# Second mixer: high parts of most weights written by rounding transfers, and the turns of a tile's last head moved into the projection ahead of it

## The chip, the cores and the metric

The kernel runs on one core of one Trainium2 chip. The metric is the time of one execution on the device, in microseconds; of several runs the median counts. The engines of a core are named as in its profile: PE is TensorE's matmul and PEld its loading of weights (PE's stationary operand), DVE is VectorE, ACT is ScalarE, POOL is GpSimd, and SP is SyncE, which here only issues transfers. Every engine works through its own queue of instructions; semaphores tie the queues together.

## The reference

Two groups of requests, 256 and 512 rows of width 1024, go through the same two layers. Layer 0 mixes the tokens by windowed attention, layer 1 by differential attention, and each mixer is followed by a SwiGLU part. Norms stand before and behind every part. Cut to what matters here, the second mixer is:

```python
def diff_attention(h, w_in, w_o, ..., subln_g, lambda_init):
    qkv = h @ w_in                                  # 1024 x 3072
    q, k, v = split(qkv)                            # 8 heads: two q and k of 64 each, one v of 128
    q, k = apply_rope(q) * HEAD_DIM ** -0.5, apply_rope(k)
    p = softmax(q @ k.T)                            # for both halves of a head
    a = p[:, :, 0] - lam * p[:, :, 1]
    o = rms_norm(a @ v, subln_g) * (1.0 - lambda_init)
    return o @ w_o                                  # 1024 x 1024

x = x + rms_norm(diff_attention(rms_norm(x, g_pre), ...), g_post)
x = x + rms_norm(swiglu(rms_norm(x, ...), ...), ...)
```

Everything is in float32, and all of the keys of a group are seen by each of its queries.

## The kernel before

**Products in two parts.** A float32 product is made of three products in the rounded format fp32r. Each operand is kept as a high part (the value rounded) and a low part (the value less its high part); `product_steps` (L367 on) issues hi x hi, hi x lo and lo x hi into one bank, lines L376 to L378. One step is three matmuls.

**Weights.** A list of units, `units`, names every block of weights in the order of its use, a block being 128 x 1024 in most cases. `plain` (L185) puts a block in the list. `fetch` loads its raw copy (SP, two buffers `wraw`), and `prepare` makes the two parts, `whi` and `wlo`, in rings of five buffers each (`RING`). A high part can come in two ways. Most are made by `two_parts` (L272): ACT casts the raw copy (L273) and DVE subtracts (L274). Units 4 to 13, nine of the first mixer's `waf` and its first block of `wo`, are written by a transfer that POOL issues from the tensor in HBM straight into `whi` (L321); it rounds on the way, and DVE then subtracts as before (L322), from the raw copy that is still loaded. `take` hands out prepared units in order, and `free(n_live)` prepares as many more as the ring holds, each as soon as the last matmul that read its buffer is done. A unit is therefore prepared while four others lie ready or are in use.

**The second mixer**, `mixer_b`. The rows are cut into six tiles of 128, tiles 0 and 1 of the first group and 2 to 5 of the second. `b_fill` lists the products in their order: q and k of a head (two halves of 384 columns each, 24 matmuls a half), and the values in three groups of heads (six tiles each). In the list of units the first q, k and value group come first, then q and k of heads 1 and 2, value group 1 (four units of 128 x 768), q and k of heads 3 to 5, value group 2 (four such units), q and k of heads 6 and 7, then eight units of `wo`, four for each half of its columns. Behind the last use of a unit stands a `drop`, which frees it and prepares another. `rotate` (L653 on) turns the result of a product by rotary positions: ACT copies it out of its bank (L657), POOL swaps neighbouring rows by two transfers (L659), DVE multiplies and adds (L661, L664, L665), and ACT and DVE place the two parts (q: L672, L674; k: L679, L681, and a transfer by POOL at L682). This rest of the work is issued at the end of the next product.

The attention of a head and a tile is three events, set between the steps of the products at places written out by hand: `score` (PE L1017, maxima on DVE L1021, exponentials on ACT L1023, the combination of both softmaxes on DVE L1026 to L1031), two events later `turn_e` (four or two transposes `tpa` on PE L1059, copied by ACT L1061), and one more event later `values` (PE L1072; ACT L1076 scales, L1078 squares). With the last of heads 3, 6 and 7 of a tile the outputs are scaled by their norm on POOL (L421, L1085). `turn_heads` then transposes finished heads for the projection (PE L1043, tile `tp_o`) and splits them in two parts (ACT L1046, DVE L1047); a tile has three such turns, for heads 0 to 3, 4 to 6 and 7.

**The projection.** `out_unit` makes the eight steps of a tile by one half of `wo` and an `end`, which sums squares and applies the gain. In `mixer_b` the last nine scores are interleaved by hand with the steps of tiles 0 to 2 (`run`). Its last entry is the turn of head 7 of tile 3. `project` then does tiles 3 to 5 of the first half, with `turn_o(t + 1)`, the turn of head 7 of the next tile, issued ahead of tile t, and after that all six tiles of the second half, each followed by its norm.

## Time and profile before

| | us |
|---|---|
| three runs | 1639.44, 1642.69, 1642.81 |
| median | 1642.69 |
| the profiled execution | 1643.67 |
| its span, first to last instruction | 1641.9 |
| granted clock of TensorE, mean | 0.998 |

| stage (from the start of the span) | us |
|---|---|
| products of the second mixer, first `pqb` to last `pkb` | 774 to 1050 |
| projection, tiles 0 to 2 with heads 6 and 7 | 1050 to 1093 |
| projection, the rest, and entry of the feed-forward part | 1093 to 1161 |

The page gives busy times by engine over the whole span. A view of stretches gives the same for chosen windows; a view of waits gives, for each engine, which instruction stood idle and what released it; groups put together the instructions of one line and tile; and the timeline gives them one by one: start, length, engine, line, operation, tile written and tiles read, shape, and in brackets the engine's idle time ahead of it with what ended it. A PE row's length holds its passage through the array, so rows overlap; the distance between two starts is what a matmul costs.

### The profile page before, as it was taken

To read this page: it belongs to the slowest core of one execution; us is meant where nothing else is said; L and a number is where in the kernel's file an instruction comes from. 1 tells how busy PE (TensorE), PEld (TensorE's weight loads), DVE (VectorE), ACT (ScalarE), POOL (GpSimd) and SP (SyncE) were. 2 spreads that over 40 slices of the span, in tenths; PEclk is the share of its full clock that TensorE was granted. 3 is DMA by queue.
4 is the path that set the end of the run, shared out by engine and by line. 5 is a ranking of instruction groups with operands and counts; after the bars stand their busy time and mean duration, and the time that the engine had idled before them with its cause. 6 is when DMAs were issued, how large, how long until landed. Compare 5 with 4: busy or idle time off the path is not lost. (4 is left out here: it accounts for less than half of the span.)

```text
span 1641.9 us, 24431 instructions
## 1 busy us (share of the span) xinstructions
PE 1610.2 (98%) x9055; PEld 1491.5 (91%) x9055; DVE 1200.9 (73%) x2076; ACT 941.0 (57%) x1999; POOL 170.9 (10%) x261
## 2 busy tenths in 40 slices
PE   7999999999999999999999999999999999999998
PEld 7888878989999998888999999888999999998887
DVE  6778857886667656988595886847886677656986
ACT  6588976644444444556475666766644444444553
POOL 1121101000000000001220250421000000000000
PEclk9999999999999999999999999999999999999999
DMA  6532204543432347675432332504544332437665
GB/s 213 173 99 68 97 14 170 177 149 133 134 117 97 125 135 251 223 270 179 144 109 73 95 85 79 153 1 164 171 152 141 123 122 96 132 126 255 225 234 175
DMA packets 73383, 233.07 MB, mean 142 GB/s; under 512 B 9072, under 2 KB 17456, under 8 KB 73008
## 3 DMA queue, kind: packets, MB, share of 16 engines
q1 hardware_dynamic: 55008, 178.82, 32.3%
q0 software_dynamic: 18112, 52.44, 10.6%
q8 instruction: 71, 1.16, 0.3%
q14 instruction: 48, 0.39, 0.1%
q10 hardware_dynamic: 144, 0.26, 0.0%
HBM read 171.71 MB, written 42.86 MB: 131 GB/s over the span
## 5 line engine op out<-in xcount | busy, mean ns | idle before, releaser
L274 DVE TENSOR_TENSOR wlo<-wraw,whi 128x1024 fp32r<-128x1024 f32 (+1 forms) x161 | 190.7, 1188 | 188.4 <-ACT whi L273 187.4
L273 ACT CAST whi<-wraw 128x1024 fp32r<-128x1024 f32 (+1 forms) x161 | 164.3, 1024 | 130.7 <-PE py L377 61.5
L376 PE MATMUL py<-hhi,whi 128*128 128x384 f32 x480 | 161.4, 337 | 1.7 <-ACT u L1183 1.2
L378 PE MATMUL py<-hhi,wlo 128*128 128x384 f32 x480 | 160.4, 334 | 0.0
L377 PE MATMUL py<-hlo,whi 128*128 128x384 f32 x480 | 160.4, 334 | 0.0
L364 ACT CAST hhi<-araw 128x768 fp32r<-128x768 f32 (+1 forms) x74 | 57.5, 782 | 94.9 <-DMA araw<-act 94.5
L376 PEld LDWEIGHTS py<-hhi,whi 128*128 128x128 f32 x480 | 90.1, 188 | 4.4 <-ACT u L1183 2.6
L378 PE MATMUL pv<-whi,hlo 128*128 128x512 f32 (+1 forms) x240 | 92.2, 384 | 0.4 <-DVE hlo L365 0.4
L376 PE MATMUL pv<-whi,hhi 128*128 128x512 f32 (+1 forms) x240 | 92.3, 384 | 0.0
L377 PE MATMUL pv<-wlo,hhi 128*128 128x512 f32 (+1 forms) x240 | 92.1, 384 | 0.0
L377 PEld LDWEIGHTS py<-hlo,whi 128*128 128x128 f32 x480 | 90.1, 188 | 0.0
L378 PEld LDWEIGHTS py<-hhi,wlo 128*128 128x128 f32 x480 | 90.1, 188 | 0.0
L365 DVE TENSOR_TENSOR hlo<-araw,hhi 128x768 fp32r<-128x768 f32 (+1 forms) x74 | 65.2, 889 | 34.0 <-ACT hhi L364 33.6
L1226 POOL DMA_DIRECT2D act<-st x22 | 19.3, 879 | 629.4 <-DVE st L1225 599.2
L376 PE MATMUL po<-whi,hhi 128*128 128x512 f32 x192 | 78.5, 409 | 0.0
L1023 ACT ACTIVATE be<-bsc,bmx 128x512 f32<-128x512 f32 (+1 forms) x96 | 58.8, 616 | 29.9 <-DVE bmx L1021 29.5
L377 PE MATMUL px<-hlo,whi 128*128 128x384 f32 x224 | 75.0, 335 | 0.5 <-DVE hlo L365 0.5
L376 PE MATMUL px<-hhi,whi 128*128 128x384 f32 x224 | 75.4, 337 | 0.0
L377 PE MATMUL po<-wlo,hhi 128*128 128x512 f32 x192 | 75.2, 392 | 0.0
L378 PE MATMUL po<-whi,hlo 128*128 128x512 f32 x192 | 75.2, 392 | 0.0
L378 PE MATMUL px<-hhi,wlo 128*128 128x384 f32 x224 | 75.0, 335 | 0.0
L1021 DVE TENSOR_REDUCE bmx<-bsc 128x1 f32<-128x512 f32 (+1 forms) x96 | 55.2, 593 | 11.5 <-PE bsc L1017 11.2
(318 smaller groups left out, 4920.3 us busy)
## 6 DMA issues: line engine op xcount, KB each, us to landing
wraw<-in_wgu SPq DMA_DIRECT2D x60, 512.0 KB, 4.4
act<-st POOLq DMA_DIRECT2D x22, 1344.0 KB, 6.6
araw<-act SPq DMA_DIRECT2D x70, 384.0 KB, 4.0
y_wraw<-in_wgu SPq DMA_DIRECT2D x40, 512.0 KB, 3.6
wraw<-in_wd SPq DMA_DIRECT2D x40, 512.0 KB, 4.0
xd<-x SPq DMA_DIRECT2D x18, 512.0 KB, 2.9
x<-xd SPq DMA_DIRECT2D x18, 512.0 KB, 4.1
wraw<-in_wo SPq DMA_DIRECT2D x16, 512.0 KB, 3.5
```

The source lines that it names most:

```text
L273: state["raw_hi"] = nc.scalar.copy(out=hi, in_=src)
L274: state["raw_lo"] = nc.vector.tensor_tensor(out=lo, in0=src, in1=hi.bitcast(F32), op=ALU.subtract)
L364: state["hi"] = nc.scalar.copy(out=hi, in_=src)
L365: state["lo"] = nc.vector.tensor_tensor(out=lo, in0=src, in1=hi.bitcast(F32), op=ALU.subtract)
L376: nc.tensor.matmul(out, ah, bh, start=start and i == 0, stop=False, skip_group_check=more)
L377: nc.tensor.matmul(out, ah, bl, start=False, stop=False, skip_group_check=more)
L378: state["mm"] = nc.tensor.matmul(out, al, bh, start=False, stop=stop and i == last, skip_group_check=more)
L1021: nc.vector.tensor_reduce(out=mx, in_=s, axis=AX.X, op=ALU.max, negate=True)
L1023: nc.scalar.activation(out=e[:, :n * P], in_=s, func=AF.Exp, bias=mx, accum_out=den[:, c:c + 1])
L1226: nc.gpsimd.dma_start(out=at_hand[c // 4][:, :, c // 2 % 2], in_=out.pop(c // 2))
```

## The change

`plain` takes a flag that puts the unit in a set, `cast`, and `prepare` asks that set instead of the bounds 4 and 14. The flag is set for the first mixer's `waf` and its first `wo` block, as before by the bounds, and now also for `wb` and `wbv` with n > 0 (q and k of heads 1 to 7, value groups 1 and 2) and for the four blocks of the first half of the second mixer's `wo`. In `project` the turn of the next tile's last head is issued behind the first five steps of a tile, not ahead of them; the first mixer passes no such turns.

```diff
-N_PLAIN_A = 14
...
-    def plain(src, n):
+    cast = set()
+
+    def plain(src, n, rounded=False):
+        if rounded:
+            cast.add(len(units))
         units.append(("plain", len(raw_src), n))
         raw_src.append((src, n, "w"))
...
     for f in dict.fromkeys(u for kind, u, _ in a_fill() if kind != "kv"):
-        plain(waf[f], 1024)
+        plain(waf[f], 1024, True)
     for n2 in range(2):
         for i in range(4):
-            plain(wo[0, n2, i], 1024)
+            plain(wo[0, n2, i], 1024, n2 == 0 and i == 0)
...
                 w = 2 * HALF if V_HEADS[n] == 3 else D
-                plain(wbv[n, i, :, :w], w)
+                plain(wbv[n, i, :, :w], w, n > 0)
         else:
-            plain(wb[n, "qk".index(kind)], D)
+            plain(wb[n, "qk".index(kind)], D, n > 0)
     for n2 in range(2):
         for i in range(4):
-            plain(wo[1, n2, i], 1024)
+            plain(wo[1, n2, i], 1024, n2 == 0)
...
-                if 4 <= i < N_PLAIN_A:
+                if i in cast:
                     nc.gpsimd.dma_start(out=hi[:, :n], in_=raw_src[r][0])
...
         for t in range(done, NT):
-            if turn_o is not None and t + 1 < NT:
-                for s in turn_o(t + 1):
-                    s()
-            for s in out_unit(t, wk, o, 0, gp, sq, f"po{layer}_0_{t}"):
+            out = out_unit(t, wk, o, 0, gp, sq, f"po{layer}_0_{t}")
+            for s in out[:5] + (turn_o(t + 1) if turn_o is not None and t + 1 < NT else []) + out[5:]:
                 s()
```

## The prediction

> **What bounds the kernel now.** I read the first part of the page first, then the stretches of time around the second mixer, then who TensorE waited for there.

> ```profile
> span 1641.9 us, 24431 instructions
> PE 1610.2 (98%) x9055; PEld 1491.5 (91%) x9055; DVE 1200.9 (73%) x2076; ACT 941.0 (57%) x1999; POOL 170.9 (10%) x261
> ...
> 774.00:1050.00 276.00, 276.00 (x1759) 269.96 (x1759) 203.73 (x386) 174.98 (x458) 69.27 (x107) 1.00 0.35 102
> 1050.00:1093.00 43.00, 41.53 (x260) 35.31 (x258) 33.85 (x73) 38.21 (x124) 18.40 (x24) 1.00 0.28 82
> ...
> PE tp_h L498 <- DVE y_po L431: 1.4, 1, 1.4
> PE tp_o L1043 <- POOL ob L1085: 1.3, 1, 1.3
> PE tpa L1059 <- ACT be L1023: 0.5, 1, 0.5
> PE tpa L1059 <- ACT aT L1061: 0.5, 1, 0.5
> PE px L377 <- DVE hlo L365: 0.5, 1, 0.5
> PE tpa L1059 <- DVE be L1031: 0.4, 1, 0.4
> ```

> TensorE is busy for 98% of the span, so the end moves only by what TensorE stands idle. The rows of stretches give their length, then the busy time of PE, PEld, DVE, ACT and POOL, the granted clock, and the DMA share. From 774 to 1050 us the second mixer's query, key and value products run with the attention of heads 0 to 5 between them: PE is busy for 276.00 of 276.00 us. From 1050 to 1093 us (heads 6 and 7 among the first three tiles of the output projection; I call it the tail) it idles 1.47 us. The six waits are all that PE had between 770 and 1175 us, in total, times and longest; the second stands behind the tail, in the projection of tiles 3 and 4, the first and the fifth lie behind the projection, at the entry of the feed-forward part. What the change can win is therefore the 1.3 us of `tp_o` and at most the 1.4 us of the three `tpa`.

> **Part one: 26 weights are rounded on the way in.** The new set adds to the second mixer 14 blocks of `wb` (q and k of heads 1 to 7), 8 of `wbv` (groups 1 and 2) and 4 of `wo`. The first mixer keeps its ten: nine `waf` and one `wo`, as with the old bounds 4 to 13. Each of the 26 loses a cast on ACT and gains a transfer issued by POOL; the subtraction on DVE stays (L274 becomes L322).

> ```profile
> L273 ACT CAST whi<-wraw 128x1024 fp32r<-128x1024 f32 x21 | 22.0, 1049 | 12.2 <-PE pvb L378 5.6 <-DMA wraw<-in_wb 2.9 <-PE pqb L377 2.5
> L273 ACT CAST whi<-wraw 128x768 fp32r<-128x768 f32 x8 | 6.7, 832 | 5.3 <-PE pkb L377 4.3 <-PE pqb L377 1.0
> L274 DVE TENSOR_TENSOR wlo<-wraw,whi 128x1024 fp32r<-128x1024 f32 (+1 forms) x29 | 33.1, 1149 | 21.8 <-ACT whi L273 21.6
> ...
> L321 POOL DMA_DIRECT2D whi<-in_waf x9: 530/553/716, 12.6 to 111.6; - x9
>   DVE wlo L322: 5.1, 5
>   PE pqa L376: 0.5, 1
> DMA to landing us min/median/max: 3.8/5.1/5.8
> ```

> The first three rows are groups of 770 to 1060 us (first two) and 770 to 1100 us (third), with count, busy time, mean in ns and idle time before. Of the 29 casts, three stay (two `wbv` of group 0 and the first `wo` of the second half), so ACT loses 18 x 1.049 + 8 x 0.832 = 25.5 us. The value to the end is zero: PE has no idle time in 774 to 1050, where nearly all of these casts lie.

> What part one adds is lateness. The last four rows are the same transfer in the first mixer: 0.553 us to issue, 3.8 to 5.8 us to land, DVE waiting for it or its raw copy 5 times for 5.1 us in all, and PE once for 0.5 us. Before, the wait stood on ACT: 12.2 + 5.3 us of idle time ahead of the casts. Now POOL stands waiting for PE to leave the buffer. Queued behind it there is the rotation's swap of rows of the same product (L659), which waits for that product's end anyway, and then loses only the issue, 0.55 us. Behind the waiting subtraction on DVE stand the maxima (L1021) and combinations (L1031) of the scores, and PE's transposes `tpa` wait for those. How much they can lose:

> ```profile
> 837.32 0.75 DVE L1031 SCALAR_TENSOR_TENSOR be<-be,rho 128x512 f32<-128x512 f32 x1
> 839.17 0.60 PE L1059 MATMUL tpa<-ident,be 128*128 128x128 f32 x4
> ...
> 892.86 0.48 DVE L1031 SCALAR_TENSOR_TENSOR be<-be,rho 128x256 f32<-128x256 f32 x1
> 903.62 0.38 PE L1059 MATMUL tpa<-ident,be 128*128 128x128 f32 x2
> ...
> 1042.48 1.05 ACT L273 CAST whi<-wraw 128x1024 fp32r<-128x1024 f32 x1
> 1051.30 1.03 ACT L273 CAST whi<-wraw 128x1024 fp32r<-128x1024 f32 x1
> 1053.51 0.74 DVE L1031 SCALAR_TENSOR_TENSOR be<-be,rho 128x512 f32<-128x512 f32 x1
> 1054.40 0.63 PE L1059 MATMUL tpa<-ident,be 128*128 128x128 f32 x4 [0.48 <-ACT aT L1061]
> ```

> The columns are start, length, engine, line. The first pair has the least room that I found in the fills: 838.07 to 839.17, 1.1 us. The second stands where value group 1 ends and four buffers come free within some 5 us, so four transfers come together: 893.34 to 903.62, 10.3 us. In the tail there is none: 1054.25 to 1054.40. Of the 26 only one is prepared close to it, the fourth `wo` block, behind the last products of q of head 7 (the cast at 1042.48); the cast inside it, at 1051.30, belongs to the first block of the second half, which stays on ACT. Weights themselves are in no hurry, since a block is prepared while four others are in the ring of five. From nine transfers with 5.1 us of waits I take 0.6 us of DVE waiting for each of the 26 (estimate), against the 21.6 us that DVE now waits for ACT. Bounds: DVE's saving shows as the three `tpa` waits gone, -1.4 us; or each transfer costs PE what the first mixer's rows allow at worst (the rival below), +7.5 us. I take 0, the rows of 774 to 1050.

> [...]

> **Part two: the turns of a tile's last head.** Before, `turn_o(4)` is issued ahead of tile 3's projection. The rows around it:

> ```profile
> 1092.85 0.27 PE L1043 MATMUL tp_o<-ident,ob 128*128 128x128 f32 x1
> 1094.46 0.33 PE L1043 MATMUL tp_o<-ident,ob 128*128 128x128 f32 x1 [1.33 <-POOL ob L1085]
> 1094.54 0.48 PE L376 MATMUL po<-whi,hhi 128*128 128x512 f32 x1
> 1094.86 0.40 PE L377 MATMUL po<-wlo,hhi 128*128 128x512 f32 x1
> 1095.10 0.40 PE L378 MATMUL po<-whi,hlo 128*128 128x512 f32 x1
> ...
> 1100.12 0.27 PE L1043 MATMUL tp_o<-ident,ob 128*128 128x128 f32 x1
> ...
> 1094.00 0.40 POOL L1085 TENSOR_TENSOR ob<-ob,rstd_sub 128x128 f32<-128x128 f32 x1
> ...
> 1092.28 0.62 DVE L1047 SCALAR_TENSOR_TENSOR hlo<-tp_o,subl,hhi 128x384 fp32r<-128x384 f32 x1 [0.60 <-ACT hhi L1046]
> 1094.03 0.35 DVE L1047 SCALAR_TENSOR_TENSOR hlo<-tp_o,subl,hhi 128x128 fp32r<-128x128 f32 x1 [0.19 <-ACT hhi L1046]
> ```

> PE turns tile 3's head 7 at 1092.85, then stands until POOL has scaled tile 4's head 7 (1094.00 + 0.40 = 1094.40). From one transpose to the next are 1.61 us; a follower in a row of `tpa` (4 in 0.60 us, one lasting 0.27) comes after 0.11, so the wait costs 1.50 us. With five steps of tile 3 ahead, 15 products at 0.24 us (1094.86 to 1095.10), PE goes on at 1093 and reaches the turn at about 1096.6, two us after its data. What is late next? Steps 4 to 6 read heads whose low parts end at 1092.90, step 7 a part that ends at 1094.38; these are reached at about 1095.9 and 1098.0, after 12 and 21 products. The bank of `po` is now taken before that of the turn, the number of banks is the same. `turn_o(5)` moves too, but at 1100.12 it did not wait. Moving costs one more change from transposes to products: the first product behind a transpose takes 0.32 us to its follower (1094.54 to 1094.86), the next 0.24; estimate +0.08. The turn's instructions (a weight load and a transpose on PE, L1046 on ACT, L1047 on DVE) stay the same, and no DMA is among them. Sum: -1.50 + 0.08 = -1.4 us. Bounds: 0 (something else of tile 3 is late by as much) and -1.6.

> **Sum.** The profiled execution took 1643.67 us, of which 1641.9 is the span and 1.77 lies around it: 1643.67 - 1.4 = 1642.3. It lies 0.98 above the median of the runs shown, 1642.69, so against that median 1642.69 - 1.4 = **1641.3 us**, 0.09% less. A measurement of this kernel can tell about 0.2%, 3.3 us, from no change.

> **Rivals.**
> 1. *ACT's relief reaches the tail.* The chain through 1053.51 is fed by ACT and DVE, and both are nearly full there (38.21 and 33.85 of 43.00 us). A cast and a wait less before 1050 could clear all three `tpa` waits: 1641.3 - 1.4 = 1639.9. For it: the cast at 1042.48 goes. Against it: DVE's work stays the same and the cast at 1051.30 remains.
> 2. *The projection of tile 3 waits for something else*, so that the moved turn wins nothing: 1642.7. Against it: the rows above end in time.
> 3. *Slower: the subtraction blocks DVE until the transfer lands.* DVE runs its queue in order. In the first mixer the same transfers went with these waits of PE, between 40 and 130 us:

> ```profile
> PE tpe L830 <- DVE y_e L812: 2.1, 1, 2.1
> ...
> PE pqa L376 <- DMA whi<-in_waf: 0.5, 1, 0.5
> ...
> 70.97 1.22 DVE L322 TENSOR_TENSOR wlo<-wraw,whi 128x1024 fp32r<-128x1024 f32 x1
> ```

> The second is a wait for the transfer itself; the first came behind a subtraction that DVE ran from 70.97 to 72.19. Together they are 2.6 us on nine transfers; 26 of them would give 26 x 2.6 / 9 = 7.5 us, so 1641.3 + 7.5 = 1648.8. The place is the tail (the transfer behind the last q, landing near 1046) and the two bursts of four; it decides as soon as DVE is held for longer than the room of its `tpa`, 1.1 us at the least in the fills, nothing in the tail. Against it: in the fills the room is 1.1 to 10.3 us, and the subtraction at 70.97 had no wait of its own ahead of it.
> 4. *The change does not do what it says for the end*: the rotations' swaps, on the same POOL queue, land later. Its rows, issue and landing of the q's swaps, and the scores that read the last of them:

> ```profile
> L659 POOL DMA_DIRECT2D xqb<-xqb x32: 545/567/642, 781.3 to 1044.8; - x32
> DMA to landing us min/median/max: 1.8/2.6/4.6
> ...
> 1073.48 1.18 PE L1017 MATMUL bsc<-kb,qb 128*128 128x512 f32 x4
> ```

> They take 1.8 to 4.6 us already; the last is issued at 1044.8 and read at 1073.48, so 5 us more cost nothing, and the time stays that of the forecast, 1641.3.

> [...]

> **How the numbers follow.** The forecast (part two wins 1.4, part one is hidden) 0.55, with a range of its own of 1639.4 to 1643.0, as wide as the runs of before lie apart (1639.44 to 1642.81). Rival 1 0.13, rival 2 0.10, rival 3 0.20, rival 4 0.02. Faster by over 0.2% needs 1639.4 or less: two fifths of rival 1 and the lower end of the forecast, 0.05 each, so 0.10. Slower by over 0.2% needs 1646.0: three quarters of rival 3, 0.15. The rest, 0.75, is no change. The range of 8 in 10 reaches from 1638.6 (rival 1 less the spread of the runs) to 1647.5 (rival 3 at four fifths of its price); about 0.05 lies below it and 0.10 above.

> **What would show it.** Right: no wait of `tp_o` for POOL; casts of weights on ACT between 770 and 1060 down from 29 to 3; L322 on DVE waiting for `whi` about 15 us in all; PE still full from 774 to 1050; the three `tpa` waits still there. Wrong: new waits of `tpa` or `bsc` on DVE after L322, PE waiting for `whi` itself, or the `tpa` waits gone.

## The result and the profile after

| | median us (runs) | ratio to before, 95% interval |
|---|---|---|
| before | 1641.2 (7) | |
| after | 1651.2 (7) | 1.0053 [1.0040, 1.0066] |
| after, measured again beside the experiments | 1650.5 (6) | 1.0057 [1.0035, 1.0079] |

The change makes the kernel slower by 10 us between the medians, 8.7 us by the ratio. The forecast was 1641.3, no change. The two profiled executions lie only 4.5 us apart: that of before took 1643.67 us, 2.5 more than the median of its kernel, that of after 1648.13, 3 less than its own. Part of this arises ahead of the change: in the fourteen profiles of this document the second mixer's products begin anywhere from 770.9 to 779.0 us, before at 774.5 and after at 771.4. What the change costs is therefore read from lengths inside the second mixer, not from the ends of the two profiles.

Where it goes is seen first in the same stretches of time as before the change (length, then busy time of PE, PEld, DVE, ACT, POOL, granted clock, DMA share, GB/s):

```profile
774.00:1050.00 276.00, 271.19 (x1714) 264.05 (x1713) 194.09 (x372) 144.17 (x415) 79.52 (x129) 0.99 0.48 143
1050.00:1093.00 43.00, 40.41 (x248) 34.25 (x246) 35.72 (x78) 36.10 (x114) 18.70 (x24) 1.00 0.34 102
```

ACT has lost its casts (174.98 to 144.17 us), the DMA engines are busier (0.35 to 0.48), and PE, full before, now stands for 4.8 us in the first stretch and gets 45 matmuls fewer done. Its clock is 0.99 there, not 1.00. The boundaries of a stage move with such stalls, so I compare lengths from first to first matmul of a kind. The tile view gives them (duration in ns, then first and last start): products from the first `pqb` to the first `po`.

```profile
L376 PE MATMUL pqb<-hhi,whi x128: 333/334/423, 774.5 to 1040.6; 128*128 128x384 f32 x128
L376 PE MATMUL po<-whi,hhi x96: 387/389/482, 1051.1 to 1146.7; 128*128 128x512 f32 x96
```

```profile
L379 PE MATMUL pqb<-hhi,whi x128: 333/334/423, 771.4 to 1044.9; 128*128 128x384 f32 x128
L379 PE MATMUL po<-whi,hhi x96: 388/389/499, 1056.6 to 1152.4; 128*128 128x512 f32 x96
```

The products (with the attention of heads 0 to 5 in them) take 276.6 us before and 285.2 after, 8.6 us more: the loss lies there. From the first `po` to the feed-forward part's first `px` are 96.3 us before (1051.1 to 1147.4) and 96.5 after (1056.6 to 1153.1): nothing won. (Lines of the changed kernel stand three further down than those of before as far as `project`, one further behind it.) PE's waits of 770 to 1175 us after, total, times, longest:

```profile
PE bsc L1018 <- DMA kb<-kb: 2.3, 2, 1.7
PE pob L1073 <- ACT be L1024: 1.7, 1, 1.7
PE tpa L1060 <- DVE be L1032: 1.6, 3, 0.8
PE tpa L1060 <- DVE rden L1027: 0.8, 1, 0.8
PE pob L1073 <- ACT aT L1062: 0.6, 1, 0.6
PE po L380 <- DVE wlo L277: 0.6, 1, 0.6
PE po L379 <- ACT be L1024: 0.4, 1, 0.4
PE tp_h L501 <- DVE y_po L434: 0.4, 1, 0.4
```

The wait of `tp_o` for POOL is gone, as forecast. What that wins is lost again behind the products: the tail (here from the first `po` to the turn of head 7 of tile 3) takes 42.6 us where it took 41.8, and once, near 1121 us, PE waits 0.6 us for a low part. New are three waits inside the products: 0.8 us at 837, 2.3 us at 926 and 927 (scores of head 3 waiting for the copies of its own k), and 1.7 us at 986. Who was late is told by DVE's queue: what stood idle ahead of the subtraction `wlo` and until when, in the tile's view of 770 to 1070.

```profile
L325 DVE TENSOR_TENSOR wlo<-wraw,whi x26: 941/1224/1696, 780.1 to 1051.3; 128x1024 fp32r<-128x1024 f32 x18, 128x768 fp32r<-128x768 f32 x8
...
  DMA wraw<-in_wb: 10.0, 3
  issue: 8.9, 1
  DMA whi<-in_wb: 8.9, 7
  DMA whi<-in_wbv: 3.9, 3
```

The rounding transfers in the same view, from issue to landing:

```profile
DMA to landing us min/median/max: 3.3/4.1/7.4
```

DVE stands 22.8 us at these subtractions for transfers: 8.9 + 3.9 = 12.8 for the rounding transfer, 10.0 for the raw copy. (The row `issue` is a wait for which the view finds no releaser, of 8.9 us ahead of the subtraction at 802.6; its transfer was issued at 798.7. Directly behind it stands only the next subtraction, which waits for a transfer of its own, so I leave it out of the sum.) The wait at 837 follows such a hold (DVE, then PE):

```profile
824.46 0.96 DVE L325 TENSOR_TENSOR wlo<-wraw,whi 128x768 fp32r<-128x768 f32 x1 [2.32 <-DMA whi<-in_wbv]
...
836.37 0.75 DVE L1032 SCALAR_TENSOR_TENSOR be<-be,rho 128x512 f32<-128x512 f32 x1
...
837.27 0.63 PE L1060 MATMUL tpa<-ident,be 128*128 128x128 f32 x4 [0.81 <-DVE rden L1027]
```

This is the very pair that the prediction showed as its least room, 1.1 us between a combination at 837.32 and its `tpa` at 839.17. Counted from the first `pqb` the combination now comes 2.2 us later (836.37 - 771.4 against 837.32 - 774.5), after a hold of 2.32 us, and the room is gone. The worst place is the group of four transfers at the end of value group 1. DVE's timeline there:

```profile
889.92 1.23 DVE L325 TENSOR_TENSOR wlo<-wraw,whi 128x1024 fp32r<-128x1024 f32 x1 [1.20 <-DMA whi<-in_wb]
891.92 1.22 DVE L325 TENSOR_TENSOR wlo<-wraw,whi 128x1024 fp32r<-128x1024 f32 x1
898.49 1.23 DVE L325 TENSOR_TENSOR wlo<-wraw,whi 128x1024 fp32r<-128x1024 f32 x1 [5.36 <-DMA wraw<-in_wb]
...
907.45 0.56 DVE L667 TENSOR_TENSOR xqb<-xqb,rope 128x384 f32<-128x384 f32 x1 [2.15 <-DMA xqb<-xqb]
```

There are two raw buffers. The first two subtractions end at 891.15 and 893.14, later than they would without the wait for `whi`; only then do the third and fourth raw loads start (891.2 and 893.2), in the midst of the transfers, and take 7.2 and 6.3 us to land, where the raw loads of the kernel before took 3.5 in the middle and 4.2 at most (870 to 910 us). The subtraction behind stands 5.36 us, and the rotations behind that one meet a queue of their own: four swaps issued from 902.7 to 904.9 take 4.1 to 4.7 us (1.8 to 1.9 before). So k of head 3 is placed late. The copies of `kb` before (tile view), and the scores that read them (timeline):

```profile
L682 POOL DMA_DIRECT2D kb<-kb x2: 602/604/606, 920.5 to 921.1; - x2
DMA to landing us min/median/max: 2.7/3.1/3.5
```

```profile
926.10 0.63 PE L1017 MATMUL bsc<-kb,qb 128*128 128x256 f32 x4
```

and both views after:

```profile
L685 POOL DMA_DIRECT2D kb<-kb x2: 600/608/616, 922.2 to 922.8; - x2
DMA to landing us min/median/max: 3.7/3.9/4.2
```

```profile
926.08 0.47 PE L1018 MATMUL bsc<-kb,qb 128*128 128x256 f32 x2 [1.70 <-DMA kb<-kb]
927.14 0.77 PE L1018 MATMUL bsc<-kb,qb 128*128 128x256 f32 x2 [0.59 <-DMA kb<-kb]
```

Before, the second copy landed at 921.1 + 3.5 = 924.6 and was read at 926.10: a room of 1.5 us. After, counted from the first `pqb`, the copies are issued 922.25 - 771.4 = 150.9 us in, against 920.5 - 774.5 = 146.0: 4.9 us later, and the room is gone. That stall brings a second loss behind it (the granted clock is the third column from the right):

```profile
925.00:930.00 5.00, 3.33 (x15) 3.19 (x16) 3.58 (x9) 2.97 (x8) 2.86 (x5) 0.69 0.74 143
930.00:935.00 5.00, 5.00 (x34) 5.00 (x33) 3.61 (x8) 2.21 (x7) 0.57 (x2) 0.96 0.42 121
```

PE's waits in the products are 5.2 us (0.8 + 2.3 + 1.7, and 0.4 ahead of the first `po`), and matmuls at half clock cost some 1.7 more (last section). The other 1.7 of the 8.6 us are not accounted for.

### The profile page after: what moved, and what is told of

It reads as the page before. It is cut to its first block, busy times and chain, and to the rows that moved or that the text cites. A ratio compares the mean times of both kernels' runs of the same rounds, so it can differ in the third digit from the quotient of the medians.

```text
span 1646.4 us, 24439 instructions
## 1 busy us (share of the span) xinstructions
PE 1611.5 (98%) x9055; PEld 1491.1 (91%) x9055; DVE 1200.4 (73%) x2076; ACT 917.1 (56%) x1973; POOL 178.3 (11%) x287
## 5 line engine op out<-in xcount | busy, mean ns | idle before, releaser
L277 DVE TENSOR_TENSOR wlo<-wraw,whi 128x1024 fp32r<-128x1024 f32 (+1 forms) x135 | 161.2, 1197 | 164.3 <-ACT whi L276 163.5
L276 ACT CAST whi<-wraw 128x1024 fp32r<-128x1024 f32 (+1 forms) x135 | 138.9, 1032 | 106.4 <-PE py L380 61.5
L1024 ACT ACTIVATE be<-bsc,bmx 128x512 f32<-128x512 f32 (+1 forms) x96 | 58.7, 616 | 63.8 <-DVE bmx L1022 63.4
L325 DVE TENSOR_TENSOR wlo<-wraw,whi 128x1024 fp32r<-128x1024 f32 (+1 forms) x36 | 42.3, 1176 | 38.8 <-DMA wraw<-in_wb 10.0
```

Source lines behind the costliest of these rows:

```text
L276: state["raw_hi"] = nc.scalar.copy(out=hi, in_=src)
L277: state["raw_lo"] = nc.vector.tensor_tensor(out=lo, in0=src, in1=hi.bitcast(F32), op=ALU.subtract)
L325: state["raw_lo"] = nc.vector.tensor_tensor(out=lo[:, :n], in0=src[:, :n], in1=hi[:, :n].bitcast(F32), op=ALU.subtract)
L1024: nc.scalar.activation(out=e[:, :n * P], in_=s, func=AF.Exp, bias=mx, accum_out=den[:, c:c + 1])
```

## The experiments

Two theories stood after these traces. **Theory 1**: DVE is held, because its queue runs in order and the subtraction stands in it until its transfer (and in groups the raw copy) has landed. **Theory 2**: each weight now crosses the DMA engines twice, and this traffic slows swaps and raw loads; DVE's wait is a bystander. Twelve runs followed. "Products" is the stretch from the first `pqb` to the first `po` in the profile, "rest" that to the first `px`; before has 276.6 and 96.3. Both come from one profiled execution of each run.

| run | median us (runs) | ratio to before, 95% interval | products | rest |
|---|---|---|---|---|
| e1, turns only | 1640.5 (12) | 0.9995 [0.9983, 1.0008] | 276.6 | 94.9 |
| e2, rounding only | 1648.7 (6) | 1.0046 [1.0030, 1.0061] | 283.5 | 98.3 |
| e3, all 26, subtracted a fill later | 1651.1 (8) | 1.0048 [1.0030, 1.0066] | 280.8 | 100.2 |
| e4, 18 single transfers | 1645.5 (12) | 1.0022 [1.0009, 1.0034] | 280.1 | 95.7 |
| e5, all 26, no raw loads | 1645.1 (11) | 1.0025 [1.0014, 1.0035] | 279.8 | 96.3 |
| e6, traffic alone | 1642.5 (12) | 1.0006 [0.9995, 1.0017] | 279.2 | 95.2 |
| e7, 18 single, a fill later | 1643.8 (12) | 1.0017 [1.0003, 1.0031] | 276.8 | 99.1 |
| e8, 15 single, a fill later | 1641.1 (12) | 1.0000 [0.9988, 1.0013] | 276.6 | 96.0 |
| e9, groups of four alone | 1643.1 (12) | 1.0010 [0.9999, 1.0021] | 279.3 | 96.8 |
| e10, groups, no raw loads | 1639.5 (12) | 1.0000 [0.9986, 1.0013] | 276.7 | 95.8 |
| e11, the 15 of e8, at once | 1645.2 (12) | 1.0025 [1.0011, 1.0039] | 279.7 | 96.5 |
| e12, the change again | 1650.5 (6) | 1.0057 [1.0035, 1.0079] | 283.1 | 96.8 |

Before, run beside them, had medians of 1640.4 to 1641.1. No run is told from it on the faster side.

**e1 and e2: one part each.** e1 is the kernel before with the change's `project`, e2 the changed kernel with the old one. The edit of e2 against the changed kernel:

```diff
-            out = out_unit(t, wk, o, 0, gp, sq, f"po{layer}_0_{t}")
-            for s in out[:5] + (turn_o(t + 1) if turn_o is not None and t + 1 < NT else []) + out[5:]:
+            if turn_o is not None and t + 1 < NT:
+                for s in turn_o(t + 1):
+                    s()
+            for s in out_unit(t, wk, o, 0, gp, sq, f"po{layer}_0_{t}"):
                 s()
```

> The kernel before with part two alone: the turns of a tile's last head inside the projection of the tile ahead; all 29 roundings of second-mixer weights stay copies on ScalarE. What the prediction's step says: the 1.50 us wait of tp_o for POOL goes, 0.08 us of a wait for hlo comes, -1.4 us, so 1639.8 beside 1641.2 for the kernel before (ratio 0.9991). If the whole loss sits in the second mixer's products, this run has none of it: its poB-to-px2 stretch is 1.4 us shorter than before and its pqb-to-poB stretch is that of before, 276.6 us. If the moved turns themselves cost something (they now sit behind ScalarE's and VectorE's work of the tile ahead), the run is above 1641.2 and the tail or the projection is the longer stretch.

> The changed kernel with the turns where they were before: the 26 rounding transfers alone. Theory 1 (VectorE is held by its in-order queue until each transfer has landed) and theory 2 (the transfers slow the swaps and raw loads on the DMA engines) both give the whole loss and the part-two gain taken back: 1651.2 + 1.4 = 1652.6 (ratio to before about 1.007), the second mixer's products at 285 us against 276.6. If the loss needed both parts together, this run would lie near 1641.

The loss belongs to the transfers. The turns alone leave the products at 276.6 and shorten the rest by 1.4 us (96.3 to 94.9), the forecast term; the time, 0.9995, neither proves nor denies 1.4 us. e2's time is 3.9 us under the 1652.6 expected (1648.7), on six runs. In its profile the stalls at 837 and 986 come back (0.8 us at 839, 1.7 at 984), the one for `kb` near 925 does not; there is one of 1.6 us at 1046 in its place. (The expectation of e12 has these stalls some 0.16 us longer than the profile's waits; here and below the waits are given.)

**e3 and e4: defer the subtraction, or leave the groups out.**

```diff
+            if i in cast and state["defer"]:
...
+                nc.gpsimd.dma_start(out=hi[:, :n], in_=raw_src[r][0])
...
+                owed.append((i, r, n))
...
+                continue
...
                 turned(late)
+                subtract_owed(min(2, old, len(owed)))
```

`subtract_owed` fetches the raw copy and issues the subtraction behind DVE's last combination or rotation of that fill. e4 only takes the flag from k3, q4, k4, q5, k6, q7, k7 and the first `wo`.

> The changed kernel with the same 26 rounding transfers at the same places of POOL's queue, but in the second mixer each subtraction that reads the result, and the raw copy's fetch behind it, is given out at the end of the fill after the one in which the transfer was issued, and ordered behind VectorE's work of that fill. The traffic is the same (26 transfers of 393 or 524 KB, the same raw loads), the waits of VectorE for whi should fall from 12.8 us to under 3 us. Theory 1 (VectorE held): the loss goes, the products come back to 276 to 278 us and the time to 1639.8 to 1642 (ratio 0.999 to 1.001). Theory 2 (traffic slows swaps and raw loads, VectorE's wait is a bystander): the loss stays, 1647 to 1652. A time between says how it is shared.

> The changed kernel with the eight units that are prepared four in a row at the ends of value groups 1 and 2 (k3, q4, k4, q5 and k6, q7, k7 and the first of wo) rounded by ScalarE as before; the other 18 transfers stay. If every transfer costs alike, 18/26 of 10 us stay: 1641.2 - 1.4 + 18/26 x 11.4 = 1647.7. If the groups of four are what hurts (the stalls of 1.87 and 0.75 us at 924 and the slow matmuls behind them come after the group at 886 to 891, where VectorE waits 5.4 us for the raw copy), about half goes: near 1645 and no wait of the scores of head 3 for kb; the two stalls at 836 and 984, which follow single transfers, stay. If single transfers are what hurts, it stays at 1650.

e3 spoke against theory 1, on its face: the time stays. The rows say why it could not decide. No wait for `whi` is left, but DVE stands for `wraw` (timeline), and PE waits here (770 to 1175 us; these kernels' lines differ: L287 is the deferred subtraction, L1043 the scores, L1085 `tpa`):

```profile
906.50 1.23 DVE L287 TENSOR_TENSOR wlo<-wraw,whi 128x1024 fp32r<-128x1024 f32 x1 [1.08 <-DMA wraw<-in_wb]
...
911.39 1.23 DVE L287 TENSOR_TENSOR wlo<-wraw,whi 128x1024 fp32r<-128x1024 f32 x1 [3.00 <-DMA wraw<-in_wb]
```

```profile
PE tpa L1085 <- ACT be L1049: 4.4, 1, 4.4
PE bsc L1043 <- DMA kb<-kb: 2.1, 2, 1.1
```

A subtraction that comes later frees its raw buffer later; the raw loads now meet the transfer issued at 902.8 and the swaps (7.7 to 8.0 us to land), and `kb` is late again. The 4.4 us lie in the tail, where the deferral itself reordered DVE's queue (rest 100.2; e8 below, which defers nothing of `wo`, has no such wait). e4 halves the loss, 5.0 us over e1, with the stalls near 841 and 986 (0.8 and 1.6 us) and no wait for `kb`. So both kinds of transfer cost, and each needed a run in which only one thing differs.

**e5, e6, e7: held without the traffic, traffic without the holding, single transfers deferred.** e5 skips the raw loads and reads the high part twice; e6 is e1 with, for each of the 26,

```diff
+                    at = nc.gpsimd.memset(lo[:, :1].bitcast(F32), 0.0)
+                    spare = dram.tile([P, 1028], F32R, name=f"spare{i}")
+                    with tc.issue_after(at.ins):
+                        nc.gpsimd.dma_start(out=spare[:, :n], in_=raw_src[r][0])
```

and e7 is e4 and e3 together.

> The changed kernel without SP's raw loads of the 26 second-mixer weights: the subtraction reads the high part twice, so the low parts are zero (the correction of the weights is left out). Each weight now crosses the DMA engines once, as before the change, while VectorE's subtraction still stands in its queue until the rounding transfer has landed. Theory 1 (VectorE held): the waits of wlo for whi stay near 12.8 us and the loss stays for the most part, 1647 to 1651. Theory 2 (twice the traffic slows swaps and loads): the transfers land in about 3.3 us, the swaps in 1.8 us, and the loss goes, 1640 to 1643.

> The kernel before with part two, plus 26 extra transfers that nothing waits for: at the place of each rounding transfer in POOL's queue, released by the same slot of the ring (a one-column fill of the low part's tile stands ahead of it), the same weight goes from DRAM to a spare place in DRAM. The roundings stay copies on ScalarE, so VectorE waits for no transfer of them. Theory 1: nothing happens, 1640.5 (ratio 0.9985 to 1.0005). Theory 2: the extra traffic slows swaps (4 to 8 us instead of 1.8) and raw loads, and the loss is that of the change, 1646 to 1651.

> The 18 transfers of the run without groups of four, and each of their subtractions a fill later, as in the run that deferred all 26. That deferred run lost its waits for whi and kept its loss, with the raw copies still landing together with a transfer after the group of four (8.2 us for the raw copy, 8.0 us for a swap) and VectorE waiting 4.1 us for them; here that collision can't happen. The run without groups was 1645.5, 5 us over the turns alone (1640.5), with 10.6 us of VectorE's waits for whi. Theory 1: those 5 us are the held VectorE, and the deferral takes them: 1640.5 to 1642. Theory 2: the 18 transfers cost by their traffic alone, and 1645.5 stays.

None came out as one theory had it. e5 loses 4 us: the waits for `kb` are gone and so is the one at 837, the stall at 984 stays (1.7 us, `pob` for `be`) while DVE waits 15.8 + 2.5 + 1.4 = 19.7 us for `whi` (the view of the tile `wlo`; 7.5 us of it are the wait that after the change stands as `issue`):

```profile
  DMA whi<-in_wb: 15.8, 10
  DMA whi<-in_wbv: 2.5, 3
...
  DMA whi<-in_wo: 1.4, 3
```

e6 has its transfers in flight for 3.2 to 8.9 us each and no wait for `kb`; its ratio, 1.0006, is 1 us, with an interval that holds no change; its products are 2.6 us longer, but DVE waited 4.8 us for POOL's one-column fill, which the experiment had brought in, so not all of this is the traffic's. Its transfers also end in DRAM and not in the weights' buffers, so it is no exact copy of the change's traffic. Its swaps of q do land as late as after the change (3.4 us in the middle here, 3.3 after the change, and 5.0 at most in both; 2.6 and 4.6 before), and yet no `kb` is waited for. e7 has the products back at 276.8 with the traffic of its 18 transfers unchanged; what it loses it loses in the tail (99.1), by the deferral's reordering, as e3 did.

**e8 and e11: the same 15 transfers, deferred and not.** e8 is e7 without the three of `wo`, e11 the changed kernel with the same 15 flags. The transfers stand at the same places of POOL's queue, and from the projection on the orders are alike.

> The run of 18 single transfers with deferred subtractions, less the three of wo, so 15 transfers; from the projection on, every engine's order is that of the turns alone. The run of 18 had its second-mixer products back at 276.8 us (276.6 before) and lost 4.2 us in the tail (46.0 against 41.8), at one 3.8 us wait of tpa for be behind a rotation that VectorE's changed order put ahead of the scores. If that order was the deferral's own accident, this run is the turns alone, 1640.5 (ratio 0.9985 to 1.0005), products 276.6 to 277, tail 41.7. It then also says what 14.7 us of ScalarE's copies are worth when nobody is held: nothing. If ScalarE's relief is worth something it is under 1639; if transfers cost by themselves it stays near 1643.8.

> The partner of the run of 15 deferred transfers (1641.1): the same 15 roundings of q, k and v by transfer, each subtraction where the change puts it, at once behind its transfer; wo and the groups of four by ScalarE. Only the place of the subtraction in VectorE's order differs. If the held VectorE is the cost of single transfers, this run shows the stalls near 836 to 841 (about 1 us) and 984 (1.8 us) of the run of 18 single transfers, its products are 279.5 to 280.5 against 276.6, and its time 1644 to 1645.5. If the 5 us of that run came from the three transfers of wo, it is 1641 with products of 276.6.

This pair decides for single transfers: 1641.1 against 1645.2 us, products 276.6 against 279.7, the same transfers and the same ACT. The place is seen in the timeline (DVE, then PE), of e11:

```profile
967.91 0.48 DVE L1032 SCALAR_TENSOR_TENSOR be<-be,rho 128x256 f32<-128x256 f32 x1
971.34 1.44 DVE L325 TENSOR_TENSOR wlo<-wraw,whi 128x1024 fp32r<-128x1024 f32 x1 [2.95 <-DMA whi<-in_wb]
972.69 1.13 DVE L684 TENSOR_TENSOR kb<-zkb,kb 64x384 fp32r<-64x384 f32 x2
973.85 1.29 DVE L1022 TENSOR_REDUCE bmx<-bsc 128x1 f32<-128x512 f32 x2
...
982.34 0.71 PE L1073 MATMUL pob<-vb,aT 128*128 128x128 f32 x4 [1.77 <-ACT be L1024]
```

and of e8:

```profile
970.58 0.48 DVE L1057 SCALAR_TENSOR_TENSOR be<-be,rho 128x256 f32<-128x256 f32 x1
970.98 1.13 DVE L708 TENSOR_TENSOR kb<-zkb,kb 64x384 fp32r<-64x384 f32 x2
972.14 1.29 DVE L1047 TENSOR_REDUCE bmx<-bsc 128x1 f32<-128x512 f32 x2
...
976.39 1.22 DVE L287 TENSOR_TENSOR wlo<-wraw,whi 128x1024 fp32r<-128x1024 f32 x1
...
981.72 0.61 PE L1098 MATMUL pob<-vb,aT 128*128 128x128 f32 x4
```

In e11 the subtraction stands 2.95 us in front of the placing of k and the next two maxima; in e8 these follow the combination at once and the subtraction comes behind them at 976.39, without a wait: its transfer was issued at 968.7 and landed 4.1 us later. Some 10 us further on, PE waits 1.77 us for an exponential (L1024) in e11 and for nothing in e8. The deferral moves one thing more, the raw load, which is fetched together with its subtraction. e5 has no raw loads and keeps the stall at 984 (1.7 us), so that one is the held queue's. The wait at 837 is gone in e5, where DVE was held 1.87 us at that place and not 2.32, so there the raw loads have a share. e8 also answers what the casts were worth: 15 are off ACT and the time is 1.0000 of before, where e1, with the same turns and all casts on ACT, has 0.9995.

**e9 and e10: the groups of four, with and without the raw loads.**

> Turns plus the eight transfers of the two groups of four alone, the other 18 roundings by ScalarE: the complement of the run without groups. If the two kinds add, this run is 1640.5 + (1651.2 - 1645.5) = 1646.2, with the wait of the scores of head 3 for kb (2.3 us in two pieces near 924) in its products and no stall near 836 or 984. If the groups only hurt because the single transfers ahead of them had eaten the room, it is near 1641 and has no kb wait.

> The groups alone, without SP's raw loads of these eight weights (their subtraction reads the high part twice, so their low parts are zero). The run without any raw loads kept its stall near 982 (1.7 us, after a single transfer) and had no kb wait, though VectorE still waited for whi. If the groups' loss needs the second raw buffer's load that the late subtraction sets off in the middle of the transfers (5.4 us of VectorE's wait for wraw), this run has no kb wait and is 1640.5 to 1641.5. If the held VectorE alone makes the kb wait, it stays at 1646.

Alone, the groups cost 2.6 us over e1 where 5.7 was expected. Their wait for `kb` came, but at 1040 (0.7 us), behind the second group, not at 926: without the single transfers the copies of head 3 were in time. DVE waited 5.3 us for `wraw`. Without the raw loads all of that is gone (products 276.7, 1639.5 us). So in the groups, by these profiles, the loss needs the second half of the chain, a raw buffer freed late and refilled in the midst of the transfers; DVE's wait for `whi` alone (2.6 us in e10) costs nothing there. The times do not show it: the intervals of e9 and e10 overlap and both hold 1. The profiles may also show too much, since e9's is of one of its slowest executions (1646.5 us) and e10's of one of its fastest (1637.9).

**e12: the change again.**

> The changed kernel, a second time: the time is 1650 to 1652 again. Its profile says which stalls belong to the change and which to one execution: the profiled execution before had 0.97 us near 837, 2.62 us for kb near 925, 1.85 us at 984; the rounding alone had 1.00 at 839 and 1.89 at 984, none at 925 and 1.76 at 1046. Held VectorE predicts the first and third again, at the same instructions; the kb stall comes where a margin of 1.6 us in the kernel before is used up, so it may come or not, or come at another head's k.

1650.5 us. The stalls at 841 (0.8 us) and 985 (1.8) are there for the third time, after the change's first profile and e2; `kb` waited 0.6 us near 929 and not 2.3. So the first and last belong to the change, and the middle one is a room that is used up in some executions.

What stays open: over e1 the single transfers cost 0.0027 (e4) and the groups 0.0015 (e9); with e1's own -0.0005 the sum is 0.0037, less than the change's 0.0053 to 0.0057. Each of the three has an interval of about 0.001 to either side, so a plain sum is not excluded. That the two together eat rooms which each alone leaves is what e9's missing wait at 926 suggests; no run isolates it.

## Why the prediction was wrong

**The step that failed: "The value to the end is zero", and with it "I take 0, the rows of 774 to 1050".** It took a PE that is busy for 276.00 of 276.00 us as cover. That row says that nothing was late, not by how much things may become late. The step set a mean, 0.6 us of waiting for each transfer, against a smallest room of 1.1 us; the waits that hurt came in single holds of 2.3 to 5.4 us. Measured, part one costs about 7.5 us by e2 (1.0046), and 10 by the change (1.0053) if the 1.4 us that the turns win are added; the intervals hold both. Nor does the end move "only by what TensorE stands idle": some 1.7 of the 8.6 us in the products are matmuls at half clock, which count as busy (last section).

- *The room.* It was read only from combination to `tpa`, at three places. One of them gave way: the pair with the least room, 1.1 us, is the wait at 837 (0.8 us, after a subtraction that held DVE 2.32 us at 824). The other two places were of kinds that had not been read: scores waiting for `kb`, 1.5 us of room before, and `pob` waiting for an exponential.
- *DVE's wait*, "0.6 us for each of the 26": 22.8 / 26 = 0.88 in the profile. The size was near; 10.0 of it are waits for the raw copy in the groups, which the step didn't have. The larger fault is the comparison with "the 21.6 us that DVE now waits for ACT". Waits in sum were the wrong measure: the single ones that hurt were longer than the room behind them.
- *ACT's 25.5 us are worth nothing*: right. e8 has 15 casts less and 1.0000. *Weights are in no hurry*: right, PE waited for no `whi` or `wlo` in the products, and in the projection once, for a block that ACT had cast (0.6 us); why that one was late is not shown.
- *Landing*, "3.8 to 5.8 us to land" in the first mixer: in the second it took 3.3 at the least, 4.1 in the middle and 7.4 at most, and DVE waited.
- *Part two*: its mechanism and size hold in the profile of e1 (rest 96.3 to 94.9, the wait for POOL gone). The times can't tell 1.4 us.
- *Rival 3* named the mechanism, the side and about the price (7.5 us; the loss plus part two's 1.4 is near 10), but at 0.20. That the price came near is luck: 2.1 of its 2.6 us on nine transfers are one wait of `tpe`, which the prediction itself could not tie to a held subtraction. Of its places the tail lost under 1 us and the first burst of four did give way, though at `bsc` and not at `tpa`. Its counter-argument, "in the fills the room is 1.1 to 10.3 us", was the same short reading of the room.
- *The signs*: the casts fell to 3, the wait of `tp_o` for POOL is gone, and DVE's waits for `whi` are 12.8 us where about 15 were named. PE is not full, and new waits of `tpa` and `bsc`, a sign of being wrong, are there.
- *Rival 4* was judged by the last q alone. The swaps did become slower (4.1 to 4.7 us where they had been 1.8 to 1.9), and late rotations reached PE through k of head 3.

## What to carry to other kernels

On an engine that runs its queue in order (DVE in e11: 2.95 us idle ahead of one subtraction, and the placing of k behind it), an instruction that reads a transfer should be issued where that transfer has certainly landed: the same 15 transfers cost 4 us with the subtraction right behind the issue (e11, 1.0025) and nothing with it one fill later (e8, 1.0000). A bound engine at 100% is no cover for lateness (PE, busy for 276.00 of 276.00 us before, had 5.2 us of waits in the products after): list the smallest room of every kind of edge that feeds it (here combination to transpose, placed k to scores, exponential to bank), not of one. And where few buffers are refilled as their readers finish, a late reader moves the refill into the traffic that made it late (here two raw buffers, whose loads at 891.2 and 893.2 took 7.2 and 6.3 us where 3.5 had been the middle).

## What the runs showed of the hardware

**A stall of PE of about 2 us can cost 1.7 us more than itself, and where it falls decides.** All fourteen profiles have a wait of `tpe` for DVE near 74 us, at the same place in the kernel, of 1.96 to 2.08 us (2.8 in e6). In the first profile of the changed kernel it was 1.99 us, and the stretch behind it went at full clock (timeline, then the stretch with its granted clock, third from the right):

```profile
73.80 0.63 PE L833 MATMUL tpe<-ident,y_e 128*128 128x128 f32 x4 [1.99 <-DVE y_e L815]
```

```profile
73.61:77.02 3.41, 3.22 (x21) 2.78 (x23) 3.17 (x13) 3.36 (x10) 1.17 (x2) 1.00 0.37 142
```

In e12, the same kernel, it was 1.98 us:

```profile
74.19 0.68 PE L833 MATMUL tpe<-ident,y_e 128*128 128x128 f32 x4 [1.98 <-DVE y_e L815]
```

```profile
74.63:78.04 3.41, 3.41 (x14) 3.32 (x13) 2.82 (x10) 3.30 (x10) 1.09 (x2) 0.50 0.24 88
```

With 14 matmuls instead of 21 at half the clock, 3.41 x 0.5 = 1.7 us go. So the length of a wait alone does not decide. The stretches of half clock lie on a grid. Two of e3's are these:

```profile
928.59:932.00 3.41, 3.31 (x15) 3.35 (x16) 2.92 (x7) 1.74 (x5) 2.20 (x4) 0.50 0.65 176
1065.12:1068.53 3.41, 3.27 (x14) 3.20 (x15) 2.93 (x7) 2.27 (x7) 0.00 (x0) 0.50 0.71 240
```
